# Where the operands of the matmuls begin in the on-chip memory: x^T 64 and 16 bytes past its slots, all else at multiples of 128

## The chip, the core and the metric

The kernel runs on one core of a Trainium2 chip, in one launch. The core has five engines that run side by side, each with its own queue of instructions: TensorE (matmuls, in the profile PE, and its weight loads PEld), VectorE (DVE), ScalarE (ACT), GpSimd (POOL) and SyncE (SP), which here only issues DMA transfers. They work on two on-chip memories of 128 partitions each: SBUF, which holds all operands, and PSUM, into which TensorE accumulates. The metric is the device time of one execution in microseconds; lower is better.

## The reference

Two layers of a decoder trunk on x of 512 tokens by 1024 features, in float32. Each layer is a mixer and a gated feed-forward network (FFN), each followed by a residual sum and a layer norm:

```python
for layer in range(2):
    mix = even_mixer(x, ...) if layer % 2 == 0 else odd_mixer(x, ...)
    x = layer_norm(ALPHA * x + mix, ln_mix_g[layer], ln_mix_b[layer])
    x = layer_norm(ALPHA * x + swiglu(x, ffn_w_in[layer], ffn_w_out[layer]),
                   ln_ffn_g[layer], ln_ffn_b[layer])

def swiglu(x, w_in, w_out):
    h = x @ w_in                                    # 1024 -> 2 x 2816
    return (silu(h[..., :D_FF]) * h[..., D_FF:]) @ w_out
```

The even mixer projects x to 2048 columns, puts them through a short gated convolution and a pooling over trailing windows, and projects 1024 columns back. The odd mixer projects x to queries, keys, values, forget gates and a gated convolution of 31 taps, does causal attention with the forget gates in 8 heads, and projects 1024 columns back.

## The kernel before

**Three matmuls for each product.** TensorE multiplies a streaming operand (up to 512 columns) by a stationary one (128 by 128, the "weights" of a weight load). To keep float32 accuracy, each operand is split in two parts in the format float32r, a high part and a low part whose sum it is (`split`, lines 79 to 82: ScalarE writes the high part, VectorE or GpSimd the low one). A product is then three matmuls into the same PSUM bank (`mm3`, lines 84 to 87): line 85 multiplies high by high, line 86 the stationary high part by the streaming low part, line 87 the stationary low part by the streaming high part. Most of the kernel's 5371 matmuls are of these three lines.

**Two kinds of projection.** In the projections of x (`project`, lines 143 to 149; `qk_proj`, lines 594 to 604) the streaming operand is x^T: `xh` and `xl`, the high and low parts, eight blocks of 128 features by 512 tokens. The stationary one is a block of the weights `w` (`wqh` and `wql` in attention). A triple streams xh, xl, xh. The first projections after a layer norm stream two ranges of 256 tokens. In the out-projections (`OutProj.step`, lines 239 to 246) it is the other way round: the weights stream, 512 columns wide, and the activations are stationary: `hh` and `hl` in the FFN, `y`, `yc`, `yd` and part of a `qk` tile in the mixers. The values of attention (`value_proj`) also stream weights, 256 wide, with x^T stationary.

**Weights.** All weights come from HBM in pieces of 512 KB, through a ring of three buffers (`raw`), are split, and go to a ring of eight buffers (`wt`). In the second column half of an out-projection the last row pairs stay on chip, in the stage's own tiles ("resident"), and are used token tile by token tile.

**Where tiles lie.** Tiles are taken from pools, in the order of the code: constants, then `res` (the residual stream x0 to x3, then xh and xl), `raw`, `wt`, `wk` (small work tiles), and behind them one pool for each stage (even mixer, FFN, odd mixer, FFN). Each tile takes its bytes per partition, rounded up to 32, and a pool begins where the one before it ends. The constants take 1440 bytes (11 x 128 + 32), and the small tiles of `wk` 1120 (8 x 128 + 96); xh, xl, raw and w tiles are multiples of 128. By these sizes xh, xl, the ring buffers and the work tiles begin 32 bytes past a multiple of 128, and the pools of the stages at a multiple of 128. In the even mixer a few odd sizes (2080 and 2056 bytes) put its resident weights 96 bytes past one.

**Order of the work.** TensorE's instructions stand in one queue. Loads stand in SP's queue and wait for a free buffer of the ring. In attention TensorE's order is written out by hand (`SEQ`, lines 47 and 788 to 819), and the q and k projections of the next head fill its gaps. The forget gates (`forget_gates`, lines 468 to 506) have weights of their own, `fraw`, 8 columns, loaded at line 471 and used by the matmuls of lines 479 to 482.

Of the kernel before, what the change touches and what calls it, by code (L numbers as in the profile page):

```python
# [10 lines left out]
F32 = mybir.dt.float32  # L11
F32R = mybir.dt.float32r
# [5 lines left out]
P = 128  # L18
S = 512
NT = S // P  # L20
D = 1024
KD = D // P
# [4 lines left out]
NH = 8  # L27
# [5 lines left out]
# Order of the work.  # L33
CP = 900                                    # how far behind the rest background work is scheduled
WARM = 6                                    # matmuls that raise the tensor engine's clock during the first loads
START = "x0 x1 w0G x2 x3 w1G"               # first loads: token tiles, weights (low part on GpSimd or VectorE)
SPLIT = [(0, 256), (256, 512)]              # token ranges of the first projections after a layer norm
FIRST = 2                                   # FFN column pairs done by those ranges
DFIRST = 2                                  # gated linear unit tiles done by those ranges
DG = 1                                      # from this tile on, GpSimd makes the low part of the weights  # L40
XA = 2                                      # of four blocks of x^T, those that ScalarE scales
XN = 6                                      # FFN column pair at which the residual stream is completed
XG = (3, 8)                                 # attention step and place at which it is completed
FPOS = 3                                    # gated linear unit tile after which the forget gates come
GT = (0, 31, 0, 4)                          # taps of each convolution tile on ScalarE and GpSimd
PRE = "C Q0 A0 Q1 V00 V01 A1 V10 V11"       # before attention: cumulated gates, q and k, values
SEQ = "S0 F0 T0 S1 S2 F1 F2 W T1 F3"        # attention step: scores, fill, transposes, weighted values
CS = [(4, 0), (4, 6), (5, 0), (5, 6)]       # step and place of the convolution's layer norm, by token tile
CW = [(6, 1), (6, 3), (6, 7), (6, 9)]       # step and place of its activation, by channel tile
ZV = "VVAA"                                 # engine of a part of that  # L50
LAST = "-- 00 01 10 11 20 21 --"            # fills of the last two steps: output projection, row pair and tile
PIECES = [(896, 1024), (0, 512), (512, 896)]    # columns of the last layer norm; the first by ScalarE and GpSimd
# [3 lines left out]
def trunk(ctx, tc, x, ev_w_in, ev_conv_w, ev_pool_w, ev_pool_scale, ev_w_out, od_w_in,  # L56
# [4 lines left out]
    const = pool("const")  # L61
    res = pool("res")
# [16 lines left out]
    def split(hi, lo, src, eng=None):  # L79
        """hi + lo == src, each exact in float32r."""  # L80
        nc.scalar.activation(hi, src, AF.Copy)  # L81
        (eng or nc.vector).tensor_tensor(lo, src, f32(hi), op=ALU.subtract)  # L82
# [24 lines left out]
    # ---- residual stream, its transpose, constants  # L107
    xs = [res.tile([P, D], F32, tag=f"x{t}", name=f"x{t}") for t in range(NT)]
    xh = res.tile([P, KD, S], F32R, tag="xh", name="xh")
    xl = res.tile([P, KD, S], F32R, tag="xl", name="xl")  # L110
# [10 lines left out]
    def transpose_x(t, gbt=None, tags=("tp", "tp")):  # L121
        """x^T, from x or, with gbt = (g, b) by feature, from the normalised x."""
        for half in range(2):
            tp = psum(tags[half])
            for j in range(4):
                k = half * 4 + j
                nc.tensor.transpose(tp[:, j * P:(j + 1) * P], xs[t][:, k * P:(k + 1) * P], ident)  # L127
            src = tp
            if gbt is not None:
                src = wk.tile([P, S], F32, tag="sg", name="xt")  # L130
                for j in range(4):
                    k = half * 4 + j
                    blk = slice(j * P, (j + 1) * P)
                    if j < XA:
                        nc.scalar.activation(src[:, blk], tp[:, blk], AF.Identity,
                                             scale=gbt[:, 0, k:k + 1], bias=gbt[:, 1, k:k + 1])
                    else:
                        nc.vector.tensor_scalar(src[:, blk], tp[:, blk], gbt[:, 0, k:k + 1], gbt[:, 1, k:k + 1],
                                                op0=ALU.mult, op1=ALU.add)
            dst = (slice(None), slice(half * 4, half * 4 + 4), slice(t * P, (t + 1) * P))  # L140
            split(xh[dst], xl[dst], src.rearrange("p (j q) -> p j q", q=P))

    def project(accs, ws, ranges):
        """accs[i][:, tokens] = (x @ W[:, column tile i])^T, by token ranges."""
        for a, b in ranges:
            for acc, (wh, wl) in zip(accs, ws):
                for k in range(KD):
                    mm3(acc[:, a:b], wh[:, k, :], wl[:, k, :], xh[:, k, a:b], xl[:, k, a:b],
                        k == 0, k == KD - 1)
# [4 lines left out]
    # ---- layer norm of the residual stream  # L154
# [21 lines left out]
    def ln_params():  # L176
        """g and b of the three inner layer norms, by feature."""
        rows = wk.tile([6 * KD, S], F32, tag="sg", name="rows")[:, :P]
        for i, (g, b) in enumerate(((ln_mix_g[0], ln_mix_b[0]), (ln_ffn_g[0], ln_ffn_b[0]),
                                    (ln_mix_g[1], ln_mix_b[1]))):  # L180
            for n, v in enumerate((g, b)):
                nc.sync.dma_start(rows[(2 * i + n) * KD:(2 * i + n + 1) * KD, :], v.rearrange("(k p) -> k p", p=P))
        tp = tpsum()
        nc.tensor.transpose(tp[:, :6 * KD], rows, ident[:6 * KD, :6 * KD])
        nc.vector.tensor_copy(lnt, tp[:, :6 * KD].rearrange("p (i n k) -> p i n k", i=3, n=2))

    def late_affine(g, b, eng):
        """x <- x g + b after an inner layer norm, behind everything else."""
# [10 lines left out]
    def norm(t, st, gb, ln):  # L199
        """Layer norm ln; the inner ones leave the residual stream to late_affine."""  # L200
# [24 lines left out]
    class OutProj:  # L225
        """x <- LN(alpha x + lhs^T @ w); lhs(k) -> (hi, lo) [P, S]; `order` lists the row pairs; the last
        `resident` pairs of the second column half stay on chip, token tile by token tile."""
# [11 lines left out]
        def step(self, t, i, ws, part=None):  # L239
            """Row pair order[i] of token tile t; accs[t] lists (psum, columns of the half)."""  # L240
# [7 lines left out]
        def first(self, i, tokens=range(NT)):  # L248
            """Row pair order[i] of the first column half."""
# [37 lines left out]
    # ---- SwiGLU  # L287
# [30 lines left out]
    # ---- even mixer: short gated convolution and pooling  # L318
    par = const.tile([P, 4, 38], F32, tag="par", name="par")

    def params():
        """[channel, tile, row]: 0-2 conv taps, 3 pool scale, 4-34 taps, 35 dw_b, 36 cn_g, 37 cn_b."""
# [12 lines left out]
    def even_mixer():  # L335
# [5 lines left out]
        with tc.tile_pool(name="even", bufs=1) as ep:  # L341
# [12 lines left out]
            def pool_in(pu, g):  # L354
                win = 2 ** (g + 1)
                u = ep.tile([P, S + 8], F32, tag="u", name="u", bufs=2)
                nc.gpsimd.memset(u[:, 0:8], 0.0)
                nc.scalar.activation(u[:, 8:], pu, AF.Copy)
                s = u
                for i in range(g + 1):  # L360
                    n = ep.tile([P, S + 8], F32, tag="sum", name="sum", bufs=3)
# [40 lines left out]
            for j in range(4):  # L402
# [7 lines left out]
                cv = ep.tile([P, S + 2], F32, tag="cv", name="cv", bufs=2)  # L410
# [12 lines left out]
    # ---- odd mixer: forgetting attention and the convolution module  # L423
    def odd_mixer():
# [5 lines left out]
        with tc.tile_pool(name="odd", bufs=1) as op:  # L430
# [8 lines left out]
            # convolution module: gated linear unit, depthwise convolution behind everything else  # L439
            convs = op.tile([P, 4, S], F32, tag="acc", name="convs")  # L440

            def conv(hp, j):
                """Depthwise convolution; the last GT[j] taps by ScalarE and GpSimd."""
# [24 lines left out]
            def forget_gates():  # L468
                """Log sigmoid, token-major."""
                fraw = op.tile([P, KD, NH], F32, tag="fraw", name="fraw")  # L470
# [24 lines left out]
                # log1p(e) = 2 atanh(s), s = e / (2 + e) <= 1/3  # L495
# [33 lines left out]
            # values, token-major, [hi | lo] per head  # L529
# [3 lines left out]
            def value_proj(half, u, ks=range(KD)):  # L533
                """Token tiles 2u and 2u+1 of four heads' values."""
# [40 lines left out]
            # attention, head by head  # L575
# [18 lines left out]
            def qk_proj(h, ks=range(KD)):  # L594
                """q and k of head h, on partitions 0-63 and 64-127."""
# [15 lines left out]
            def operands(h):  # L611
                """0: q_hi q_lo | 1: k_hi k_hi | 2: q_hi cum 1 | 3: k_lo 1 -cum"""
# [19 lines left out]
            def softmax(h, T):  # L632
                """Three stages, for query tiles 3, then 2 and 0, then 1."""
# [24 lines left out]
            def transpose_p(pr):  # L658
                """Two stages: key tiles 0 and 1, then 2 and 3."""
# [37 lines left out]
            def conv_stats(t):  # L697
                """Layer norm over channels, token-major."""
# [12 lines left out]
            halfgb = op.tile([P, 4, 2], F32, tag="halfgb", name="halfgb")  # L711
            V.tensor_scalar(halfgb, par[:, :, 36:38], 0.5, None, op0=ALU.mult)

            def conv_swish(j):
                """z sigmoid(z) = z / 2 (1 + tanh(z / 2)), z = n g + b, channel-major."""
# [54 lines left out]
            def part_of(token):  # L770
                """Token tile of a row pair of the output projection, as "<pair><tile>"."""
# [50 lines left out]
    # ---- the trunk  # L822
# [27 lines left out]
```

## Time and profile before

| | us |
|---|---|
| median of 3 runs | 1121.96 |
| lowest and highest | 1120.37 and 1124.87 |
| span of the profiled execution | 1121.1 |
| TensorE busy (97%) | 1087.8 |
| VectorE busy (49%) | 547.2 |
| ScalarE busy (35%) | 394.7 |
| GpSimd busy (16%) | 176.4 |

The profile is of one execution; the span runs from its first to its last instruction, and the medians of the timed runs stand 0.9 us above it. The mean granted clock of TensorE is 0.991 of full speed. HBM reads are 103 MB, 94 GB/s over the span, and the 16 DMA engines are busy for about a third of it. Matmuls overlap in the pipeline: one of 512 columns is shown with 0.39 us, but the next one starts after less than that. How fast TensorE works is therefore read from the distance between starts in the timeline and not from the durations.

### The profile page before, as it was taken

How to read it: one execution, taken by the hardware profiler on the slowest of the kernel's cores; microseconds unless marked ns; L12 is line 12 of the kernel's file. 1: busy time of each engine (PE TensorE's matmuls, PEld its weight loads, DVE VectorE, ACT ScalarE, POOL GpSimd, SP SyncE). 2: the span in 40 equal slices, each digit the busy share in tenths (PEclk: the TensorE clock that was granted, in tenths of full speed). 3: DMA queues.
4: the chain of work that ended last, by engine and by line, in shares of the span. 5: the costliest groups of instructions: out<-in, count | busy, mean ns of one | idle time of the engine just before them, and what ended most of it. 6: DMA issues, size and time to landing. Idle time of an engine off the chain costs nothing.

```text
span 1121.1 us, 13500 instructions
## 1 busy us (share of the span) xinstructions
PE 1087.8 (97%) x5371; PEld 911.8 (81%) x5371; DVE 547.2 (49%) x821; ACT 394.7 (35%) x613; POOL 176.4 (16%) x160
## 2 busy tenths in 40 slices
PE   7999999999999999999998969999999999999997
PEld 7888898888888888889978757889888888888886
DVE  3845364633333322426589998564553333322426
ACT  4333134232223221224566848634232223321210
POOL 2000300000000000012697852610000000000003
PEclk9999999999999999999999989999999999999999
DMA  6433403343333222350232322323343333222312
GB/s 201 124 87 116 143 1 114 101 124 98 102 102 94 94 94 94 132 132 3 75 108 63 100 71 77 106 83 95 94 132 94 101 103 97 94 94 94 110 41 75
DMA packets 150332, 108.30 MB, mean 97 GB/s; under 512 B 5256, under 2 KB 131768, under 8 KB 150270
## 3 DMA queue, kind: packets, MB, share of 16 engines
q1 hardware_dynamic: 149648, 107.11, 32.0%
q8 instruction: 42, 0.69, 0.3%
q10 hardware_dynamic: 622, 0.34, 0.1%
q14 instruction: 20, 0.16, 0.0%
HBM read 103.17 MB, written 2.10 MB: 94 GB/s over the span
## 4 chain that ended last, share of the span: by engine, by line
PE 89%; DVE 6%; ACT 2%; DMA 1%; POOL 1%; issue 1%; SPq 0%; POOLq 0%
PE fl L85 12%; PE fl L86 12%; PE fl L87 12%; PE sc L85 9%; PE sc L87 9%; PE sc L86 9%; PE py L85 4%; PE py L86 4%; PE py L87 4%; PE cv L87 4%; PE cv L85 4%; PE cv L86 4%; DVE cv L460 2%; DVE yc L82 1%; PE tp L127 1%; DMA x<-in_x 1%
## 5 line engine op out<-in xcount | busy, mean ns | idle before, releaser
L81 ACT ACTIVATE w<-raw 128x1024 fp32r<-128x1024 f32 x176 | 185.8, 1060 | 546.9 <-PE sc L86 191.8
L82 DVE TENSOR_TENSOR w<-raw,w 128x1024 fp32r<-128x1024 f32 x148 | 180.6, 1224 | 292.8 <-ACT w L81 292.6
L86 PE MATMUL sc<-xl,w 128*128 128x512 f32 (+1 forms) x360 | 129.9, 361 | 0.0
L87 PE MATMUL sc<-xh,w 128*128 128x512 f32 (+1 forms) x360 | 129.6, 361 | 0.0
L85 PE MATMUL sc<-xh,w 128*128 128x512 f32 (+1 forms) x360 | 129.4, 362 | 0.0
L85 PE MATMUL fl<-xh,w 128*128 128x512 f32 (+1 forms) x352 | 128.6, 366 | 0.0
L86 PE MATMUL fl<-xl,w 128*128 128x512 f32 (+1 forms) x352 | 128.4, 365 | 0.0
L87 PE MATMUL fl<-xh,w 128*128 128x512 f32 (+1 forms) x352 | 128.3, 365 | 0.0
L82 POOL TENSOR_TENSOR w<-raw,w 128x1024 fp32r<-128x1024 f32 x28 | 67.6, 2423 | 212.5 <-PE fl L86 102.5
L161 POOL TENSOR_TENSOR rs<-rs,neghalf 128x1 f32<-128x1 f32 x20 | 14.5, 724 | 428.3 <-DVE rs L160 428.3
L87 PEld LDWEIGHTS sc<-xh,w 128*128 128x128 f32 x360 | 68.0, 189 | 10.4
L86 PEld LDWEIGHTS sc<-xl,w 128*128 128x128 f32 x360 | 67.9, 189 | 10.2
L85 PEld LDWEIGHTS sc<-xh,w 128*128 128x128 f32 x360 | 67.6, 189 | 10.3
L86 PEld LDWEIGHTS fl<-xl,w 128*128 128x128 f32 x352 | 66.5, 189 | 10.5
L87 PEld LDWEIGHTS fl<-xh,w 128*128 128x128 f32 x352 | 66.3, 189 | 10.7
L85 PEld LDWEIGHTS fl<-xh,w 128*128 128x128 f32 x352 | 66.4, 189 | 10.6
L86 PE MATMUL fl<-w,hh 128*128 128x512 f32 (+1 forms) x176 | 67.2, 382 | 0.0
L85 PE MATMUL fl<-w,hh 128*128 128x512 f32 (+1 forms) x176 | 67.1, 381 | 0.0
L87 PE MATMUL fl<-w,hl 128*128 128x512 f32 (+1 forms) x176 | 66.9, 381 | 0.0
L460 DVE SCALAR_TENSOR_TENSOR cv<-hp,par,cv 128x512 f32<-128x512 f32 x84 | 62.9, 749 | 5.3 <-ACT cv L448 3.9
L86 PE MATMUL py<-xl,w 128*128 128x512 f32 (+1 forms) x160 | 59.0, 368 | 0.0
L85 PE MATMUL py<-xh,w 128*128 128x512 f32 (+1 forms) x160 | 58.9, 368 | 0.0
(360 smaller groups left out, 2072.2 us busy)
## 6 DMA issues: line engine op xcount, KB each, us to landing
raw<-in_ffn_w_in SPq DMA_DIRECT2D x88, 512.0 KB
raw<-in_ffn_w_out SPq DMA_DIRECT2D x44, 512.0 KB
raw<-in_od_w_in SPq DMA_DIRECT2D x20, 512.0 KB
raw<-in_ev_w_in SPq DMA_DIRECT2D x16, 512.0 KB
raw<-in_ev_w_out SPq DMA_DIRECT2D x8, 512.0 KB
raw<-in_od_w_out SPq DMA_DIRECT2D x8, 512.0 KB
x<-in_x SPq DMA_DIRECT2D x4, 512.0 KB
qk<-qk SPq DMA_DIRECT2D x16, 128.0 KB
```

The source lines that it names most:

```text
L81: nc.scalar.activation(hi, src, AF.Copy)
L82: (eng or nc.vector).tensor_tensor(lo, src, f32(hi), op=ALU.subtract)
L85: nc.tensor.matmul(acc, lh, rh, start=start, stop=False)
L86: nc.tensor.matmul(acc, lh, rl, start=False, stop=False)
L87: nc.tensor.matmul(acc, ll, rh, start=False, stop=stop)
L127: nc.tensor.transpose(tp[:, j * P:(j + 1) * P], xs[t][:, k * P:(k + 1) * P], ident)
L161: nc.gpsimd.tensor_tensor(rs[:, 1:2], rs[:, 0:1], neghalf, op=ALU.pow)
L460: V.scalar_tensor_tensor(acc if i == KCONV - 1 else part, hp[:, i:i + S], tap(i), part, op0=ALU.mult, op1=ALU.add)
```

## The change

Five things, none of which adds an instruction to any engine's work:

- Two tiles that nothing uses are put in: `cpad`, 24 words (96 bytes), in the pool of constants, and `wpad`, 8 words (32 bytes), in `wk`. Behind them pools begin at multiples of 128 bytes.
- xh and xl get tiles 16 words (64 bytes) longer, and the parts begin `XHS` = 16 and `XLS` = 4 words into them, 64 and 16 bytes. The two lengthenings together are 128 bytes. Because xh's tile is 64 bytes longer than a multiple of 128, xl's tile begins, by the sizes, 64 bytes past one.
- Tiles of odd size in the even mixer (`u`, `sum`, `cv`) and `halfgb` in the odd one are lengthened to multiples of 128 bytes; the same elements are used.
- `fraw` gives up a tile of its own and takes a buffer of the ring `raw`, of which it uses 8 columns of each block of 128.
- Comments and docstrings are left out.

```diff
+CPAD = 24
+WPAD = 8
+XHS = 16
+XLS = 4
...
+    const.tile([P, CPAD], F32, tag="pad", name="cpad")
+    wk.tile([P, WPAD], F32, tag="pad", name="wpad", bufs=1)
...
     xs = [res.tile([P, D], F32, tag=f"x{t}", name=f"x{t}") for t in range(NT)]
-    xh = res.tile([P, KD, S], F32R, tag="xh", name="xh")
-    xl = res.tile([P, KD, S], F32R, tag="xl", name="xl")
+    shifted = lambda name, words: res.tile([P, KD * S + 16], F32R, tag=name, name=name)[
+        :, words:words + KD * S].rearrange("p (k s) -> p k s", s=S)
+    xh, xl = shifted("xh", XHS), shifted("xl", XLS)
...
-                u = ep.tile([P, S + 8], F32, tag="u", name="u", bufs=2)
+                u = ep.tile([P, S + 32], F32, tag="u", name="u", bufs=2)
                 nc.gpsimd.memset(u[:, 0:8], 0.0)
+                u = u[:, :S + 8]
...
-                    n = ep.tile([P, S + 8], F32, tag="sum", name="sum", bufs=3)
+                    n = ep.tile([P, S + 32], F32, tag="sum", name="sum", bufs=3)[:, :S + 8]
...
-                cv = ep.tile([P, S + 2], F32, tag="cv", name="cv", bufs=2)
+                cv = ep.tile([P, S + 32], F32, tag="cv", name="cv", bufs=2)[:, :S + 2]
...
-                fraw = op.tile([P, KD, NH], F32, tag="fraw", name="fraw")
+                fraw = rawp.tile([P, KD, P], F32, tag="raw", name="fraw")[:, :, :NH]
...
-            halfgb = op.tile([P, 4, 2], F32, tag="halfgb", name="halfgb")
+            halfgb = op.tile([P, 32], F32, tag="halfgb", name="halfgb")[:, :8].rearrange("p (j r) -> p j r", r=2)
```

## The prediction

> **What bounds the kernel now.** I read the page first: its span, the shares of the engines, the granted clock.
>
> ```profile
> span 1121.1 us, 13500 instructions
> PE 1087.8 (97%) x5371; PEld 911.8 (81%) x5371; DVE 547.2 (49%) x821; ACT 394.7 (35%) x613; POOL 176.4 (16%) x160
> PEclk9999999999999999999999989999999999999999
> PE 89%; DVE 6%; ACT 2%; DMA 1%; POOL 1%; issue 1%; SPq 0%; POOLq 0%
> ```
>
> TensorE is busy for 97% of the span at its full clock, and 89% of the chain that ended last is matmuls. The view by windows, one stretch for each stage, shows where that is not so (columns: stretch, its length, then busy time and count for PE, PEld, DVE, ACT and POOL, granted clock, DMA share, GB/s).
>
> ```profile
> 154.00:392.00 238.00, 238.00 (x1149) 201.26 (x1148) 95.90 (x120) 74.59 (x99) 1.82 (x3) 1.00 0.33 98
> 521.00:567.00 46.00, 46.00 (x302) 42.27 (x302) 30.53 (x51) 22.75 (x36) 30.59 (x27) 1.00 0.27 70
> 567.00:690.00 123.00, 106.07 (x623) 87.82 (x622) 110.01 (x202) 85.12 (x184) 87.11 (x67) 0.94 0.29 81
> ```
>
> The first is the first FFN's projection of x: TensorE never idles, VectorE works 96 of 238 us, ScalarE 75, and the DMA engines a third. Only attention (567 to 690 us) leaves TensorE idle, 17 us. So the end is set by the distance between the starts of successive matmuls, and the busy mean (389 ns for 512 columns) says nothing of it, since matmuls overlap. The distance is read from the timeline (columns: start in us, length, engine, line, operation, tiles, shapes). Below are seven stretches of TensorE alone; in each I show two rows of one stretch and divide the difference of their starts by the number of starts between them: 26, 26, 28, 17, 10, 26 and 11.
>
> ```profile
> 300.06 0.39 PE L85 MATMUL sc<-xh,w 128*128 128x512 f32 x1
> 305.95 0.39 PE L87 MATMUL sc<-xh,w 128*128 128x512 f32 x1
> ...
> 419.83 0.39 PE L85 MATMUL fl<-w,hh 128*128 128x512 f32 x1
> 425.92 0.40 PE L87 MATMUL fl<-w,hl 128*128 128x512 f32 x1
> ...
> 1095.63 0.39 PE L85 MATMUL cv<-w,hh 128*128 128x512 f32 x1
> 1101.98 0.39 PE L86 MATMUL fl<-w,hh 128*128 128x512 f32 x1
> ...
> 144.76 0.40 PE L87 MATMUL fl<-w,y 128*128 128x512 f32 x1
> 148.73 0.40 PE L86 MATMUL fl<-w,y 128*128 128x512 f32 x1
> ...
> 735.20 0.39 PE L85 MATMUL fl<-w,yc 128*128 128x512 f32 x1
> 737.52 0.39 PE L86 MATMUL fl<-w,yd 128*128 128x512 f32 x1
> ...
> 169.79 0.28 PE L86 MATMUL fl<-xl,w 128*128 128x256 f32 x1
> 172.91 0.28 PE L87 MATMUL sc<-xh,w 128*128 128x256 f32 x1
> ...
> 1062.19 0.28 PE L85 MATMUL fl<-w,hh 128*128 128x256 f32 x1
> 1063.48 0.28 PE L87 MATMUL sc<-w,hl 128*128 128x256 f32 x1
> ```
>
> With 512 columns this gives 226.5, 234.2, 226.8, 233.5 and 232.0 ns; with 256 columns 120.0 and 117.3 ns. The shapes of each width are alike; what differs is where the operands begin. No view shows addresses: I work them out from the tiles' sizes, laid end to end in the order of the code, each rounded up to 32 bytes. The constants end 32 bytes past a multiple of 128, so xh, xl and the streamed weights w all begin 32 past one; the pools of the stages (hh, hl, y, yc) begin at a multiple of 128, and so do the FFN's resident weights. Then:
> - streaming operand and weights at the same place (x's projections at 300 us; the resident second half at 1096 us): 226.5 and 226.8 ns, and 120.0 ns for 256 columns.
> - 32 bytes apart modulo 128 (420 us, and 145 us the other way round): 234.2 and 233.5 ns, and 117.3 ns for 256.
> - both at multiples of 128, but 128 to 384 bytes apart modulo 512 (735 us): 232.0 ns.
>
> So addresses do matter, by some 8 ns in 227, and the loss has two forms. **At the same place**, 256 more columns cost 106.5 ns (226.5 less 120.0), 0.416 ns each; 512 of them take 213.1 ns, which leaves 13.4 ns lost per matmul, and 120.0 less 106.5 leaves 13.5 ns too. The loss is the same for both widths, and at 0.416 ns a column it is the time of 32 columns, or 128 bytes of the stream. **Apart**, 256 more columns cost 116.9 ns (234.2 less 117.3), 0.457 each, with 0.4 ns left over: there the loss grows with the width.
>
> **The change part by part.** *x^T moves against its weights.* How many matmuls this concerns, from the groups by line and form (the L85 rows; lines 86 and 87 follow each of them, so a row's count is a count of triples xh, xl, xh):
>
> ```profile
> L85 PE MATMUL fl<-xh,w 128*128 128x512 f32 x272 | 105.9, 389 | 0.0
> L85 PE MATMUL sc<-xh,w 128*128 128x512 f32 x264 | 102.7, 389 | 0.0
> L85 PE MATMUL py<-xh,w 128*128 128x512 f32 x128 | 49.8, 389 | 0.0
> L85 PE MATMUL cv<-xh,w 128*128 128x512 f32 x120 | 46.7, 389 | 0.0
> L85 PE MATMUL fl<-xh,wqh 128*128 128x512 f32 x64 | 26.7, 417 | 0.0
> L85 PE MATMUL sc<-xh,w 128*128 128x256 f32 x96 | 26.7, 286 | 0.0
> L85 PE MATMUL fl<-xh,w 128*128 128x256 f32 x80 | 22.7, 287 | 0.0
> L85 PE MATMUL fl<-w,hh 128*128 128x512 f32 x154 | 60.9, 395 | 0.0
> L85 PE MATMUL sc<-w,hh 128*128 128x512 f32 x88 | 34.9, 396 | 0.0
> ```
>
> 512 columns: 272 + 264 + 128 + 120 = 784 triples, and 64 of attention's q and k. 256 columns: 96 + 80, and 48 in two smaller groups that I do not show: 224 triples.
>
> Afterwards the weights begin at a multiple of 128 and the high part 64 bytes past one. For the low part the announced place is 16; by my sum of sizes it is 80, because the high part's tile is now 64 bytes longer than a multiple of 128, so that the low part's tile begins 64 past one. Either way no pair of streaming operand and weights stands at a distance that a row above shows. Bounds, by the nearest rows:
> - worst: all of it takes the form with the growing loss: 234.2 for 226.5, +7.7 ns x 2352 matmuls = +18.1 us.
> - best: no loss is left but the 0.4 ns of that form: 213.5 for 226.5, -13 ns x 2352 = -30.6 us; and 106.9 for 120.0, -13.1 x 672 = -8.8 us.
> - the value I take lies between them. A loss that is the same for 512 and 256 columns is paid where one matmul follows another, and it is one full turn of 128 bytes. Before, all streams in a row begin at the same place within 128 bytes: if the next stream must wait until its place comes round, each junction costs a full turn. With the two parts at different places, going from xh to xl and back from xl to xh makes one turn in sum instead of two; from xh to the next xh it stays one. So each triple saves one turn of 13.4 ns, whether the parts are 48 bytes apart or 16. That is 784 x 13.4 = 10.5 us; 224 x 13.4 = 3.0 us; and 64 x 13.4 = 0.9 us in attention, of which I count half, 0.4, because TensorE idles there. Sum -13.9 us.
>
> I take this because the equal loss at both widths fits nothing but a cost per junction, and because the apart form was seen only with streams that all start at one place. It is an extrapolation, and its bounds go into the range.
>
> *Out-projections.* Streamed weights and hh, hl, y come to multiples of 128, 128 bytes apart modulo 512 by my sum; the nearest row is the one at 735 us, 232.0 for 234.2 ns. The FFNs have 154 + 88 triples from the rows above and 44 + 44 in two smaller groups, 330, less 70 resident ones: 260, or 780 matmuls; the even layer has 192. 972 x 2.2 = -2.1 us. At worst 0; at best they take the same-place form, 226.8, -7.4 x 972 = -7.2 us.
>
> *Forget gates.* Their raw weights leave a tile of their own for the ring of three raw buffers. Before, their load goes out at 520.8 us and the next load of the ring at 540.7 (timeline of SP); the first matmul that uses them starts at 567.3 (chain of work); the last row is of the list of waits: us in total, times, longest.
>
> ```profile
> 520.79 0.37 SPq L471 DMA_DIRECT2D fraw<-in_od_w_in  x1
> 540.72 0.37 SPq L92 DMA_DIRECT2D raw<-in_od_w_in  x1
> 567.32 1.61 PE py L479 x7
> ACT w L81 <- DMA raw<-in_ffn_w_in: 15.2, 6, 4.3
> ```
>
> Afterwards it waits for a buffer, and the next 512 KB load behind it on SP waits for its split. What hides this: 46 us of matmuls between issue and use. Were the cover gone, a load one place late would cost about the longest of those waits for a landing, 4.3 us. I take 0.
>
> *Padding and longer tiles* issue no instruction; the same ACT, DVE and DMA work goes to other addresses. With TensorE 2% faster, VectorE still works under half of an FFN's stretch, so nothing else is late next. I take 0; a gain or a loss of theirs would need the cover of 238 us against 96 to go.
>
> Sum: 1121.1 - 13.9 - 2.1 = 1105.1 us for the span. The median of the three runs is 1121.96, 0.9 above this execution's span; with it the forecast is **1106.0 us**. If this form of loss is right, its own range is 1100 (the out-projections take the same-place form too) to 1113 (half of the turns are saved).
>
> A rule of the Trainium skill speaks against any effect. "SBUF — State Buffer", section "SBUF: two separate sides", says that the tensor engine never waits on anyone for SBUF, and "TensorE: Matmul & The Clock Gate", section "Step-by-step: what each phase is for", gives it two independent read ports, one for the streamed operand and one for weights. By it the sum would be 0. The trace disagrees: the same shapes take 226.5 or 234.2 ns by the place of the weights alone.
>
> **The rivals.**
> - *Apart is apart.* x's projections fall into the form that grows with the width, as every seen pair with unlike places does: +18.1 us, +0.7 for q and k (half of 192 x 7.7), 672 x -2.7 = -1.8 us for 256 columns, -2.1 for the out-projections: 1121.96 + 14.9 = **1137 us**. For it: all three stretches of unlike places with 512 columns obey it, at three different distances. Against: none of them has successive streams at unlike places. It decides as soon as the distance of stream and weights, rather than of stream and stream, sets the loss. If only xh falls into it, it is two thirds of the 18.1, and 1131.
> - *The loss goes altogether.* Streams and weights out of each other's way: -30.6 - 8.8 - 1.2 (half of 192 x 13) - 2.1: **1079 us**; half of it 1101. For it: 0.4 ns of overhead is seen at 1062 us. Against: no stretch at all runs 512 columns under 226 ns. The skill's "TensorE: Matmul & The Clock Gate", section "Back-to-back issue gap", has 512 columns at 512 / 2.4 + 2.5 = 216 ns; by that the gain would be 24.7 us on the 2352. No stretch here reaches it.
> - *Nothing moves*, or the parts do not lie where they are said to lie: 16 bytes are 1.7 ns of stream, and if a junction needs more than that, the short step is missed by a turn and the triple keeps three turns. Then only the out-projections move: **1115 to 1122 us**, most likely 1120.
>
> **How the numbers follow.** My forecast's form of loss 0.31; gone altogether, or mostly, 0.13; nothing 0.17 (a quarter of it below 1116); apart is apart 0.34; a late load or a changed order, some us slower, 0.05. Half a per cent, 5.6 us, is about what a measurement of this kernel can tell from no change. Faster by more: 0.31 + 0.13 + 0.04 = 0.48. Within it: 0.13 + 0.01 = 0.14. Slower: 0.34 + 0.04 = 0.38. The range must reach both signs: from 1090, which leaves out most of the case without loss, to 1138, which leaves out what is worse than the price of 7.7 ns.
>
> **What would show it.** In the stretch of the first FFN's projection, the starts over three matmuls: 666 ns for a triple if a turn is saved, 680 if nothing moves, 702 if apart is apart, 645 or so if the loss is gone; and unequal steps within a triple, xh to xl against xl to xh, if the place of successive streams matters, equal ones if only the weights' place does. With 256 columns: 347 against 360 and 352. In the out-projections 232 against 234.2. The forecast is wrong if the steps at 256 columns get shorter while those at 512 get longer: then the loss has grown with the width.

## The result, and the profile after

The changed kernel takes 1133.16 us (median of 4 runs, 1132.57 to 1135.27), against 1122.62 us (1120.37 to 1124.87) for the kernel before on the same chip: a ratio of 1.0092, with a 95% interval of 1.0075 to 1.0109. It is slower by 0.9%; the forecast was 1106.0 us and faster. The rival "apart is apart", with 1137 us, comes closest.

The page of the changed kernel:

```profile
span 1133.5 us, 13501 instructions
PE 1099.0 (97%) x5371; PEld 909.7 (80%) x5371; DVE 549.4 (48%) x821; ACT 394.7 (35%) x613; POOL 176.6 (16%) x160
PE 89%; DVE 7%; ACT 2%; DMA 1%; issue 0%; POOL 0%; SPq 0%; POOLq 0%
```

TensorE still has 97% of the span and 89% of the chain that ended last; the span is 12.4 us longer (1121.1 before). Nothing has become late: the same matmuls run in the same order, only further apart. The view by windows shows it for the stretch of the first FFN's projection (stretch, length, busy time and count of PE, PEld, DVE, ACT, POOL, then clock, DMA share, GB/s):

```profile
154.00:392.00 238.00, 238.00 (x1128) 196.81 (x1127) 94.77 (x118) 72.79 (x97) 1.01 (x1) 1.00 0.32 95
```

1128 matmuls where there were 1149, at the same granted clock of 1.00, and TensorE busy in all 238 us of both. A busy share of 100% cannot tell a fast matmul from a slow one; the count in the window can. The timeline of TensorE gives the steps, in the same three kinds of stretch as before (start in us, length, engine, line, operation, tiles, shapes; between the two rows of a stretch lie 26, 25 and 26 steps):

```profile
299.95 0.39 PE L91 MATMUL fl<-xh,w 128*128 128x512 f32 x1
306.00 0.39 PE L93 MATMUL sc<-xh,w 128*128 128x512 f32 x1
...
420.03 0.39 PE L91 MATMUL fl<-w,hh 128*128 128x512 f32 x1
425.86 0.40 PE L92 MATMUL fl<-w,hh 128*128 128x512 f32 x1
...
170.55 0.28 PE L92 MATMUL fl<-xl,w 128*128 128x256 f32 x1
173.60 0.28 PE L92 MATMUL fl<-xl,w 128*128 128x256 f32 x1
```

| step between starts, ns | before | after | matmuls | us |
|---|---|---|---|---|
| x's projections, 512 columns | 226.5 | 232.7 | 2352 | +14.6 |
| attention's q and k, counted half | 226.5 | 232.7 | 192 | +0.6 |
| x's projections, 256 columns | 120.0 | 117.3 | 672 | -1.8 |
| out-projections | 234.2 | 233.2 | 972 | -1.0 |

The sum is 12.4 us, the growth of the span. That it fits to the tenth is luck. Added up over all starts of the two traces, and not taken from one stretch each, the first row is +13.7 us (5.8 ns a matmul), q and k are -0.4, the third row is -1.2 and the fourth -1.0. The remaining matmuls, transposes and attention's, make up +1.4, with gains and losses among them. The profiled execution is also the longest of its four, whose spans are 1130.8 to 1133.5 us: between the medians lie 10.5 us. So the steps of x's projections are the bulk of the change, and about 1 us is not resolved.

The forget gates are not among the causes. SP's timeline and the chain of work have these rows:

```profile
546.61 0.37 SPq L98 DMA_DIRECT2D raw<-in_od_w_in  x1
549.30 0.37 SPq L482 DMA_DIRECT2D fraw<-in_od_w_in  x1
```

```profile
573.54 1.62 PE py L490 x7
```

The load goes out 28.5 us later than before (549.3 against 520.8), now in turn with the other loads of the ring; but its first matmul is only 6.2 us later (573.5 against 567.3), as is all that stands around it: by then the even layer and its FFN have lost as much to the longer steps. The load has 24 us to land.

### The profile page after: what moved, and what is told of

It reads as the page before. It is cut to its first block, busy times and chain, and to the rows that moved or that the text cites. A ratio compares the mean times of both kernels' runs of the same rounds, so it can differ in the third digit from the quotient of the medians.

```text
span 1133.5 us, 13501 instructions
## 1 busy us (share of the span) xinstructions
PE 1099.0 (97%) x5371; PEld 909.7 (80%) x5371; DVE 549.4 (48%) x821; ACT 394.7 (35%) x613; POOL 176.6 (16%) x160
## 4 chain that ended last, share of the span: by engine, by line
PE 89%; DVE 7%; ACT 2%; DMA 1%; issue 0%; POOL 0%; SPq 0%; POOLq 0%
PE fl L91 12%; PE fl L92 12%; PE fl L93 11%; PE sc L92 9%; PE sc L91 9%; PE sc L93 9%; PE py L92 4%; PE py L91 4%; PE py L93 4%; PE cv L92 4%; PE cv L91 4%; PE cv L93 4%; DVE cv L471 2%; DVE yc L88 1%; PE tp L137 1%; DMA x<-in_x 1%
```

## The experiments

Three theories stood at the start. **Distance**: the place of the streaming operand against its own weights sets the step. **Junction** (the forecast's): the place of one stream against the next does. **Something else** that the change brought along: padding, the load of the forget gates, the stages' pools. In all diffs below, places and distances are in bytes, and distances are stream less weights.

### map: one distance at a time

A kernel of its own: the trunk is left out, and x is written as output. TensorE runs groups of 60 equal matmuls in a row, with nothing else to do on any engine; each group takes its streams and weights from given places.

```diff
+    for name, n, sp, wp in GROUPS:       # columns, places of the streams and of the weights by turns
+        for r in range(60):
+            a = sp[r % len(sp)] // 4 + r % 7 * 512
+            b = wp[r % len(wp)] // 4 + r % 8 * 128
+            nc.tensor.matmul(acc[:, :n], we[:, b:b + P], st[:, a:a + n], start=r == 0, stop=r == 59)
```

> A kernel of 61 groups of 60 matmuls in a row, nothing else beside them; it leaves the whole trunk out and writes x as its output. In the first 32 groups (512 columns) the streaming operand begins 0, 16, ... 496 bytes past the place of the weights modulo 512, then 16 groups of 256 columns in steps of 32 bytes, then 4, 8 and 508 bytes, then groups whose streams or weights alternate between places, then 384 and 128 columns. Theory (the distance of stream and weights modulo 512 sets the step): 226.7 ns at 0, 231 to 235 ns at every other distance, near 234 at 416, 233 at 224, 232 at 448, 234 at 464; with 256 columns 120 at 0 and 117 to 118 elsewhere; streams alternating between 64 and 80 bytes past weights at 128 give 232.6 as in the changed kernel. Rival (a turn of 128 bytes at each junction): all distances with equal streams alike, 226.7, and streams alternating between two places 222 on average. Rival (the trunk around the matmuls causes it): 216 to 227 ns everywhere.

The view of one tile, for nine of the groups (after the count: shortest, median and longest duration in ns, then the first and the last start in us, 59 steps apart):

```profile
L48 PE MATMUL sq<-st,we x60: 387/389/398, 234.4 to 247.8; 128*128 128x512 f32 x60
L48 PE MATMUL sC<-st,we x60: 388/394/398, 401.4 to 415.2; 128*128 128x512 f32 x60
L48 PE MATMUL sD<-st,we x60: 391/397/398, 415.4 to 429.3; 128*128 128x512 f32 x60
L48 PE MATMUL jb<-st,we x60: 392/394/400, 612.2 to 626.0; 128*128 128x512 f32 x60
L48 PE MATMUL jc<-st,we x60: 390/392/398, 626.2 to 639.9; 128*128 128x512 f32 x60
L48 PE MATMUL ha<-st,we x60: 278/283/283, 457.1 to 464.2; 128*128 128x256 f32 x60
L48 PE MATMUL hm<-st,we x60: 276/276/286, 499.8 to 506.5; 128*128 128x256 f32 x60
L48 PE MATMUL jf<-st,we x60: 389/389/389, 667.3 to 680.7; 128*128 128x512 f32 x60
L48 PE MATMUL wa<-st,we x60: 333/334/346, 694.5 to 704.8; 128*128 128x384 f32 x60
```

Streams 256 past the weights (sq), 64 before (sC) and 48 before (sD); the announced layout, streams at 64, 80, 64 and weights at 128 (jb); streams at 0 and 64 by turns (jc); 256 columns at the weights' place (ha) and 64 before (hm); streams at 0 and 256 by turns, with weights at 256 and 0 (jf); 384 columns at the weights' place (wa). These rows are rounded to 0.1 us. From the starts themselves, once a group has settled (its last 48 steps; in the first group, which begins slower, the last 36), in ns:

| 512 columns, distance | 0, 256 | 16 | 32 | 48 | 64 | 80 | 96 | 112 | 128 | 144 | 160 | 176 | 192 | 208 | 224 | 240 |
|---|---|---|---|---|---|---|---|---|---|---|---|---|---|---|---|---|
| step | 226.7 | 231.7 | 233.3 | 233.3 | 228.9 | 231.1 | 233.3 | 231.1 | 232.4 | 233.3 | 234.4 | 233.3 | 233.3 | 234.7 | 233.3 | 226.7 |

From 256 to 496 all sixteen values come again. At 256 columns: 120.0 at distances 0 and 96, 113.3 at 192 (64 before), 117.4 to 118.7 at the other five multiples of 32 below 256. The announced layout steps at 233.4, the streams by turns at 231.7. Four groups whose streams or weights move between 0 and 256 all step at 226.7. With 4 and 8 bytes past the weights and 4 before them 512 columns step at 235.3, 233.3 and 229.5. At 384 columns distances 0 and 32 both step at 173.3, at 128 columns both at 111.7: this loss at 32 is one of 512 columns.

So the pattern repeats after 256 bytes, not after 128, the period in which the prediction worked out places. Taken modulo 256, the same sizes of tiles put its five stretches of 512 columns at distances 0, 160, 0, 224 and (where yc is stationary) 128. There the map has 226.7, 234.4, 226.7, 233.3 and 232.4; read were 226.5, 234.2, 226.8, 233.5 and 232.0. Its two stretches of 256 columns lie at 0 and 160: 120.0 and 117.4 in the map, 120.0 and 117.3 read. A kernel of nothing but matmuls thus gives back the steps of the whole kernel.

No distance takes 512 columns faster than 226.7: there is nothing to gain on the kernel before's place. And 0 is the one place (with 240 here) where they are that fast. Streams at two places by turns gain nothing: junction has its first count against it.

### same and low64: x^T back at the weights' place, and both parts away from it

*same* is the changed kernel with x^T's tiles of exact size, which puts xh, xl and w at one place; all else of the change stays. *low64* moves the low part so that both parts stand 64 before their weights, at one place, so that no junction differs from another.

```diff
 same
-    shifted = lambda name, words: ...
-    xh, xl = shifted("xh", XHS), shifted("xl", XLS)
+    xh = res.tile([P, KD, S], F32R, tag="xh", name="xh")
+    xl = res.tile([P, KD, S], F32R, tag="xl", name="xl")
 low64
-XLS = 4
+XLS = 0
```

> The changed kernel with both parts of x^T back in tiles of exact size, so that they and the weights all lie 128 bytes past a multiple of 512; all other edits of the change stay. Distance theory: x's projections return to 226.7 ns a step, 2513 matmuls x 5.7 ns = 14 us less than the changed kernel, less 1.5 us lost at 256 columns: 1120 to 1121 us, no change against before or 0.1% faster. Rival (padding, the forget gates' load or the out-projections cost the time): stays at 1133. Junction rival: 1120 too.

> The changed kernel with the low part moved by 16 bytes, so that both parts of x^T lie 64 bytes before the weights modulo 512 and all streams begin at one place. Distance theory: still apart, some 232 ns a step for all three lines, 1130 to 1135 us. Junction rival: streams at one place pay a full turn each, 226.7 ns, 1120 us, as before.

*same*: 1120.79 us, ratio to the kernel before 0.9984 (0.9975 to 0.9993). *low64*: 1131.49 us, ratio 1.0083 (1.0064 to 1.0103). Timelines of *same* (26 steps between the rows) and of *low64* (24, and 26 at 256 columns):

```profile
300.10 0.39 PE L91 MATMUL sc<-xh,w 128*128 128x512 f32 x1
305.99 0.39 PE L93 MATMUL sc<-xh,w 128*128 128x512 f32 x1
```

```profile
300.29 0.40 PE L91 MATMUL fl<-xh,w 128*128 128x512 f32 x1
305.89 0.40 PE L91 MATMUL sc<-xh,w 128*128 128x512 f32 x1
...
170.55 0.28 PE L91 MATMUL fl<-xh,w 128*128 128x256 f32 x1
173.49 0.28 PE L91 MATMUL sc<-xh,w 128*128 128x256 f32 x1
```

226.5 ns in *same*; 233.3 and 113.1 in *low64*. With x^T back the whole loss is gone, so padding, the load of the forget gates and the new places of the stages cost nothing in sum: "something else" falls. And junction falls with *low64* as the cause of the loss: its streams all begin at one place, as those of the kernel before do, and the step is 233.3 all the same. That is the map's value for that distance (113.3 for 256 columns).

### pad64: the loss put into the kernel before

The kernel before, with one unused tile of 64 bytes between x^T and the weights' rings.

```diff
     xl = res.tile([P, KD, S], F32R, tag="xl", name="xl")
+    res.tile([P, 16], F32, tag="pad", name="pad")
```

> The kernel before with one unused tile of 64 bytes behind the low part of x^T and no other edit: weights and everything behind them move on by 64 bytes, x^T stays. Theory of the common place (the step settles at 226.7 ns only where streams and weights share one place modulo 256): x's projections leave it, 233.3 ns with 512 columns as the group at 448 in the first map has, 2513 x 6.5 = +16 us; 256 columns near 114 to 116 ns instead of 120, 660 x 5 = -3 us; the out-projections keep 32 bytes' distance: 1133 to 1136 us. If the shifted tiles, the ring's new user or the padding of the change were needed for the loss: 1122.

1134.40 us, ratio 1.0102 (1.0085 to 1.0119). The timeline, 26 steps:

```profile
299.91 0.39 PE L86 MATMUL fl<-xl,w 128*128 128x512 f32 x1
305.97 0.39 PE L85 MATMUL sc<-xh,w 128*128 128x512 f32 x1
```

233.1 ns. 64 bytes that nobody reads or writes bring the whole loss of the change: the cause is the place, and nothing that the change does.

### all_same: everything at one place

*same*, with the sizes of three more small tiles chosen so that the stationary parts of the out-projections (hh, hl, y, yc) also share the place of the streamed weights.

```diff
-    wk.tile([P, WPAD], F32, tag="pad", name="wpad", bufs=1)
...
-            self.sts = [wk.tile([P, 3, 6], F32, tag="st", name="st", bufs=5) for _ in range(NT)]
+            self.sts = [wk.tile([P, 3, 6], F32, tag="st", name="st", bufs=4) for _ in range(NT)]
...
-                u = ep.tile([P, S + 32], F32, tag="u", name="u", bufs=2)
+                u = ep.tile([P, S + 48], F32, tag="u", name="u", bufs=2)
```

> As the kernel with x^T at the weights' place, and the work tiles shortened by 128 bytes (one statistics buffer less, no padding tile) and the even stage's tiles by padding moved, so that hh, hl, y and yc too lie at the place of the weights that stream past them. Distance theory: the out-projections step from 234.2 to 226.7 ns, 972 matmuls x 7.5 ns = 7.3 us: 1113 to 1116 us, 0.6% faster than before. Rival (only x's projections are sensitive, or multiples of 128 suffice): 1120 to 1121.

1116.22 us (1115.05 to 1116.63), ratio 0.9936 (0.9922 to 0.9951): it beats both kernels. An out-projection in its timeline, 26 steps:

```profile
420.04 0.39 PE L93 MATMUL sc<-w,hl 128*128 128x512 f32 x1
425.93 0.39 PE L92 MATMUL sc<-w,hh 128*128 128x512 f32 x1
```

226.5 ns, where the kernel before has 234.2 and the changed one 233.2. Over all starts the out-projections of 512 columns take 316.1 us for the kernel before's 323.4, the 7.3 us that were forecast. What the change promised by its places is had by the opposite: not apart, but together.

### low_same: is it the distance of each matmul by itself?

The low part goes to its weights' place, the high part stays 64 before. If each matmul's step went by its own distance, line 92 would be fast.

```diff
-XLS = 4
+XLS = 16
```

> The changed kernel with the low part 48 bytes further on, at the place of the weights, the high part still 64 bytes before it. Distance theory, line by line: the matmuls that stream the low part (one in three) step at 226.7 ns, the others at 232, 1129 us in all. If one stream at a distance keeps the others from settling, all three step at 230 to 233, 1130 to 1133 us. Junction theory: high and low parts 64 bytes apart save a turn in three, 1110 us.

A miss for all three: 1137.19 us, ratio 1.0130 (1.0112 to 1.0147), the highest ratio of all. Its timeline (25 steps from the first row to the last):

```profile
300.01 0.40 PE L91 MATMUL fl<-xh,w 128*128 128x512 f32 x1
300.25 0.40 PE L92 MATMUL fl<-xl,w 128*128 128x512 f32 x1
300.48 0.39 PE L93 MATMUL fl<-xh,w 128*128 128x512 f32 x1
300.71 0.40 PE L91 MATMUL fl<-xh,w 128*128 128x512 f32 x1
...
305.87 0.40 PE L92 MATMUL sc<-xl,w 128*128 128x512 f32 x1
```

234.4 ns in the mean. Over the whole kernel the step after line 91 is 235.4, after 92, whose stream is at its weights' place, 237.5, and after 93 230.0. So the step is not a matter of one matmul's own distance either: two streams at other places keep the third from its fast step.

### map2: places that change while the distance to the next weights is 0

The map's kernel again, the trunk left out and x as output. The timeline of the changed kernel shows that the weights of a matmul are loaded while the one before it streams. Here it is line 92's, loaded from 299.95 us on, the start of line 91's matmul that the result shows:

```profile
299.95 0.19 PEld L92 LDWEIGHTS fl<-xl,w 128*128 128x128 f32 x1
```

So there are two distances: to a matmul's own weights, and to the next ones. In one row of groups the streams are at 0, s, 0 by turns, and the weights of each matmul at the place of the stream before it. The distance to the next weights, loaded meanwhile, is then 0, while that to the own weights is 0, s and -s. In another row, the place moves on by s with every matmul, in the same way; a third is in bfloat16.

```diff
+GROUPS += [("t" + LET[i], 512, (0, 16 * i, 0), (0, 0, 16 * i)) for i in range(1, 16)]
+GROUPS += [("r" + LET[i], 512, tuple(16 * i * r % 256 for r in range(16)),
+            tuple(16 * i * (r - 1) % 256 for r in range(16))) for i in range(1, 16)]
+GROUPS += [("b" + LET[i], -512, (16 * i,), (0,)) for i in range(16)]      # bfloat16
```

> Again groups of 60 matmuls in a row and nothing of the trunk; x is written as the output. Group ma: 512 columns at distance 0. Groups t: streams at places 0, s, 0 by turns, each with the next weights at its own place, so that the distance is always 0 while successive streams begin s bytes apart, s = 16 to 240. Groups u: the same with 256 columns. Groups h: 256 columns at distances of odd multiples of 16. Groups r: the place moves on by s bytes at every matmul, distance 0. Groups b: bfloat16, 512 columns, distances 0 to 240. Distance theory alone: t and r at 226.7 ns whatever s is; h between 113 and 120; b without a claim: 213 to 216 ns if two-byte streams lose nothing, else spread as float32r is. Junction theory (a full turn is waited for at each junction, hidden before because distances differed): t saves a turn in three, 222.2 ns, and r gains or loses with s, 218 to 227 ns.

Four groups in the view of one tile, 59 steps each (58 in the third): s = 64 and s = 192 of the first row, 16 bytes apart in bfloat16, and s = 96 of the second row:

```profile
L57 PE MATMUL te<-st,we x60: 388/394/396, 67.4 to 81.0; 128*128 128x512 f32 x60
L57 PE MATMUL tm<-st,we x60: 394/395/398, 178.2 to 191.9; 128*128 128x512 f32 x60
L57 PE MATMUL bb<-sb,wb x59: 379/379/379, 562.0 to 574.7; 128*128 128x512 bf16 x59
L57 PE MATMUL rg<-st,we x60: 390/390/399, 409.8 to 423.3; 128*128 128x512 f32 x60
```

In the first row every group settles between 228.9 and 233.4 ns; none reaches 226.7, though no stream is apart from the weights that are loaded beside it. In the second row the range is 228.8 to 239.2. At 256 columns the turns step at 117.0 to 120.0, and distances of odd multiples of 16 at 113.3 (at 112) to 120.0. So the distance of one matmul alone falls as the rule: that to the next weights here, that to the own weights in *low_same*. A row whose places move while each matmul keeps distance 0 to its own weights was not run. What stands so far: 512 columns are settled at 226.7 ns when all streams *and* all weights of a row share one place modulo 256. The bfloat16 groups step at 215.8 ns (the row above gives 219 over 58, one of its records being missing) at all sixteen distances: the effect belongs to float32r.

### minus16 and map3: the exception at 16 before

In the map, streams 16 bytes before their weights settled at 226.7 too, and 256 columns are shorter at some unlike places. *minus16* tries that place in *all_same*, with both parts of x^T in one tile.

```diff
-    xh = res.tile([P, KD, S], F32R, tag="xh", name="xh")
-    xl = res.tile([P, KD, S], F32R, tag="xl", name="xl")
+    xhl = res.tile([P, 2 * KD * S + 8], F32R, tag="xhl", name="xhl")
+    xh, xl = (xhl[:, i * KD * S + 4:(i + 1) * KD * S + 4].rearrange("p (k s) -> p k s", s=S) for i in range(2))
```

> The kernel with everything at one place, but x^T 16 bytes before its weights, both parts in one tile. In the first map 512 columns step at 226.7 ns there too, and in the second one 256 columns at 117.2 ns instead of 120, values (weights streaming past x^T, 16 bytes on) 116.7: 672 x 2.9 + 96 x 3.3 = 2.3 us less than with all at one place, 1113 to 1115 us. If the second place near 0 does not settle beside a busy trunk: 1128 to 1135.

A miss: 1137.23 us, ratio 1.0119 (1.0104 to 1.0134). The timeline, 25 steps, 236.8 ns, in the starts themselves 239 and 234 by turns:

```profile
299.98 0.40 PE L91 MATMUL fl<-xhl,w 128*128 128x512 f32 x1
300.22 0.40 PE L92 MATMUL fl<-xhl,w 128*128 128x512 f32 x1
...
305.90 0.40 PE L92 MATMUL sc<-xhl,w 128*128 128x512 f32 x1
```

The map has 226.7 for this distance, so the same distance has two steps. *map3* asks whether it depends on the moment at which a row begins: a first matmul of 260, 276, ... 500 columns, and then 59 equal ones (trunk left out, x as output).

```diff
+            if r == 0:
+                nc.tensor.matmul(first[:, :ahead], we[:, b:b + P], st[:, a:a + ahead], start=True, stop=True)
+            else:
+                nc.tensor.matmul(acc[:, :n], we[:, b:b + P], st[:, a:a + n], start=r == 1, stop=r == 59)
```

> The trunk's work is left out; x is written as output. 57 groups of one matmul of 260 to 512 columns and then 59 equal ones in float32r, with streams and weights at one distance in each group: 0, -16 and -64 bytes modulo 256 with 512 columns, 0 and -64 with 256. The question is whether a distance has one step or several, by the moment at which the row begins. Theory A (one step for each distance): every group of a distance settles at its map's step whatever the first matmul's length, 226.7 ns at 0 and at -16, 233.3 at -64, 120.0 and 113.3 with 256 columns. Theory B (-16 bytes has a second pattern, which it keeps when it begins at another phase): the groups at 0 all settle at 226.7, those at -16 fall into 226.7 for some first lengths and into 235 to 238 (239 and 234 by turns) for others. Theory C (every distance depends on the moment of its beginning): the groups at 0 split too.

Groups in the view of one tile (58 steps each): distance 0 after 500 columns (zp); 16 before, after 260, 276 and 372 columns (ma, mb, mh); 256 columns 64 before, after 260 and 324 (va, ve):

```profile
L51 PE MATMUL zp<-st,we x59: 389/389/397, 228.5 to 241.7; 128*128 128x512 f32 x59
L51 PE MATMUL ma<-st,we x59: 392/398/403, 242.1 to 255.8; 128*128 128x512 f32 x59
L51 PE MATMUL mb<-st,we x59: 388/388/391, 256.1 to 269.3; 128*128 128x512 f32 x59
L51 PE MATMUL mh<-st,we x59: 393/396/396, 340.2 to 353.7; 128*128 128x512 f32 x59
L51 PE MATMUL va<-st,we x59: 276/276/286, 636.2 to 642.8; 128*128 128x256 f32 x59
L51 PE MATMUL ve<-st,we x59: 281/281/282, 649.9 to 656.7; 128*128 128x256 f32 x59
```

At distance 0 all sixteen first lengths end at 226.7 ns. At 16 before, two of sixteen end at 226.7, one at 233.3, and thirteen at 236.7, in the very pattern of *minus16*. At 64 before, 512 columns end at 233.3 after every first length tried, and 256 columns at 113.3 six times and at 117.8 twice. Theory B holds (but for the one group at 233.3, which it did not foresee): some distances have several steady patterns, and which one a row settles in goes with its beginning, the first length and what ran just before it. Of the three distances tried with 512 columns, only 0 has no worse one than 226.7.

## Why the prediction was wrong

- **What bounds the kernel**: right. The steps of TensorE account for the change of the span but for about 1 us, and no other engine or load is seen to take part.
- **The addresses and the counts**: right, but for the period. The parts of x^T behave as the sum of sizes puts them, 64 and 48 bytes before their weights: the map's group at that layout steps at 233.4 ns, the stretch at 232.7. The rows "32 bytes apart modulo 128" were 160 and 224 modulo 256, two distances with two steps.
- **The step that failed** is "the value I take lies between them": that "each triple saves one turn". It rested on the sentence that a loss equal at both widths "fits nothing but a cost per junction". Its term for x^T was -13.9 us; in its place the traces have +12.1 (+13.7, -1.2 and -0.4). *low64* shows the loss where no junction changes, and the streams by turns in *map* and *map2* never gain. The split of 226.5 and 120.0 ns into a slope and a rest of 13.4 fits the shared place: 384 columns there step at 173.3, on the same line. What no row bore out was to call the rest a turn between streams that goes once they lie apart. At 64 before, the same two widths give 233.3 and 113.3: 120.0 ns for 256 columns more, and a rest of -6.7 ns. A rest below nothing is no cost of a junction; the step is a settled pattern that belongs to places and width together.
- **The sign of unequal steps** within a triple came, and points to an effect of one stream on the next, but not to a saving: 232.8, 233.9 and 231.1 ns after lines 91, 92 and 93 of the changed kernel, where *low64* has 233.3, 233.4 and 233.2.
- **The bounds**: the best case (213.5 ns) does not exist at any of the places tried; the least of all float32r groups with 512 columns is 226.7. The worst case was nearly right: 7.7 ns forecast, 6.2 measured in the stretch (5.8 over the whole kernel). The fast step was the one the kernel before already had.
- **The rival "apart is apart"**: right in sign and too large in size: 14.9 us forecast over the median, 10.5 measured between the medians (12.4 between the profiled spans). Its terms: +18.1 became +14.6 by the stretch and +13.7 over the trace, because 7.7 was the price of the out-projections, at another distance (at 64 before, the map and *low64* have 233.3, and not 234.2); -1.8 for 256 columns became -1.8 and -1.2, and q and k, +0.7, became -0.4 over the trace. Its ground was the distance from stream to weights alone, and that is not the whole rule, as *low_same* showed.
- **The out-projections**: -2.1 us forecast, -1.0 measured (233.2 ns instead of 232.0). The row at 735 us was at the right distance, 128 modulo 256; but one distance need not have one step. From 410 to 460 us, in the first FFN's out-projection, the changed kernel steps at 233.3 ns and *low64* at 232.4, with these tiles at the same places in both.
- **The forget gates and the padding**: nothing, as forecast; *same* has both and takes 0.9984 of the kernel before's time.
- **The chances**: three stretches at unlike places had been read, at three distances, and all were slower by 5.5 ns or more. They were direct evidence on the sign, and were given 0.34; the forms that went against all three had 0.44 together (0.31 for the extrapolation, 0.13 for a loss that goes altogether). The signs named for being wrong (256 columns shorter, 512 longer) are the ones that came.
- **The rule of the Trainium skill** that TensorE never waits on anyone for SBUF ("SBUF — State Buffer", section "SBUF: two separate sides"), read as a rule on its own operands too, would have made the sum 0. *pad64* disagrees with that reading: 64 unused bytes cost 1.0%.

What stays open is the mechanism inside the chip: why a place that streams and weights share is the steady one, and why a row at 16 before settles now in one pattern and now in another. The runs show when, not why. Of the places modulo 256 that all can share, three were tried: 32 in the kernel before and 128 in *same* gave 226.5 ns, 0 in the map 226.7.

## What to carry to other kernels

Where float32r matmuls of 512 columns bind, give streams and weights of a whole row of matmuls one place modulo 256 bytes, by the sizes of the tiles between them (at 256 columns other places were faster, at 384 one place beside it was as fast); a small tile put in elsewhere can break it at a cost of 1%. Read the distance between starts and the count of matmuls in a window, since busy shares and durations hide the step. Where direct rows all point one way, do not let a mechanism inferred from two numbers outvote them: measure it by itself first, in a kernel of nothing but that operation.

## What the runs showed of the hardware

- A float32r matmul of 512 columns steps at 226.7 to 239.2 ns at one granted clock, by the places of its operands and of its neighbours', and by how the row began; in bfloat16 it is 215.8 ns at all sixteen distances, near the 216 ns that "TensorE: Matmul & The Clock Gate", section "Back-to-back issue gap", of the Trainium skill gives, which float32r reaches nowhere here.
- Where the places of a float32r row stay and every step is the same, the step is a whole or a half multiple of 13.33 ns, the time of 32 columns by the 0.4167 ns a column that lies between 256, 384 and 512 columns at the shared place (120.0, 173.3, 226.7): 226.7 is 17 of them, 233.3 is 17 and a half, 120.0 is 9 and 113.3 is 8 and a half. Elsewhere the steps run through a fixed sequence, such as 239 and 234. Where the places move on with every matmul, constant steps of 229.2 and 239.2 occur too.
- At 256 columns the order is another one: the shared place gives 120.0 ns, and 64 before gives 113.3, where 512 columns lose. At 384 columns 0 and 32 past the weights both give 173.3. No single distance was the best for both widths.
